# SP's transfers in the order of emission, in a two-layer diffusion transformer on one core

## The chip, the core and the metric

The kernel runs on one core of one Trainium2 chip, in one launch. The metric is the device time of one execution in microseconds; the median of the runs counts. On a core, TensorE (PE, with its weight loads as PEld), VectorE (DVE), ScalarE (ACT) and GpSimd (POOL) compute, each from a queue of its own that it works through in order. SyncE (SP) issues all DMA transfers of this kernel, also in order: an instruction in SP's queue that waits for a semaphore holds up whatever stands behind it.

## The reference

One latent sequence of 1024 tokens and one context of 256 tokens, 1024 features each, pass through two layers; all is float32. In each layer six vectors (shift, scale and gate, twice) are made from the conditioning, `silu(c) @ ada_w + ada_b`, and then:

```
h = h + g1 * mixer(rms_norm(h) * (1 + sc1) + sh1)
h = h + g2 * swiglu_ffn(rms_norm(h) * (1 + sc2) + sh2)
```

Layer 0's mixer is neighbourhood attention with 16 heads of 64: a query on a 16 x 64 grid sees a window of 8 x 16 with a relative-position bias, and all 256 context keys. The context attends to itself and goes through the FFN too. Layer 1's mixer is grouped-query attention with 16 query and 4 key heads, norms and a rotary embedding on q and k, over all 1280 keys; here only the latent tokens go on. The FFN is `(silu(a) * g) @ w_out` with 2816 hidden features. A last norm gives the output.

## The kernel before

Features lie on the partitions, tokens along the free dimension, in three blocks: latent tokens 0 to 511 (block 0), 512 to 1023 (block 1), the context (block 2, 256 wide). Every large product is done in three passes of a rounded high part and a low part (`hi`, `lo`), so each weight tile that arrives (`wr`, 512 KB) is split in two by ACT and by DVE or POOL (lines 632 and 634). The program is written with a scheduler that places instructions by a model of their times, but over most of it the kernel itself fixes the order of the compute engines: inside `manual_schedule` an engine keeps the order in which its instructions are emitted.

There are five stages. `startup` (line 262) makes the first modulation and norm and the projections of the first head pair; its `manual_schedule` has SP in it too. Then comes the attention of layer 0, in two passes over the heads (three pairs of query tiles per head in the first, two in the second). Each pair goes through the stages S, X, m, e, sc, T, c, s, PV, oc, r and z at the times of a table (`ORDERA`, `ORDERB`, with the length of a pair in ns in `PERIODA`, `PERIODB`). In the table's slots between them (names with an F) `Lanes` puts in background work: loading and splitting weights, the Q, K and V projections of the next head pairs, the rest of layer 0's modulation (`ada_chunks`, with the tile `adaw`), and later the output projection. Then the FFN of layer 0 with layer 1's modulation behind it, the attention of layer 1 (`ORDER1`) and the FFN of layer 1 with the last norm.

The background has a clock of its own, `bg.now`, that runs by the table's times. It says when a step may be emitted: a split of a weight 2500 ns after its load was emitted, a use of `adaw` 4000 ns, of `o32` 3000 ns.

Intermediate results go through DRAM, all by `dma` (line 76), which issues on SP, so that nearly every transfer carries line 81. The ones that matter here:

- `stack_out` (line 705) stores a projected block of Q or K, its high parts and its low parts, as two transfers (`Kd<-qh`, `Kd<-ql`, `Qd<-qh`, `Qd<-ql`, in layer 1 `K1d<-`, `Q1d<-`). The destination has the head first: two heads of 64 rows. `qh` and `ql` have two buffers each. In the first attention the background projects, for head pairs 1 to 7, Q of blocks 0 and 2 and K of all three (V after pairs 2, 4 and 6), then Q of block 1 for the second pass.
- `r` (line 834) adds the two halves of a result on POOL (line 838) and, for the second head of two, moves rows between partitions by two transfers `z<-r`. `z` (line 846) adds them on POOL (lines 850, 851) and stores them, `Od<-z` or `O1d<-z`.
- `load_head` (line 1193), called in the first S of a head's second pair (line 1261), loads the next head's queries and keys (`Qs<-Qd` and six `K<-Kd` in the first pass); `load_v0` and `load_bias` load V (`Vt<-Vd`) and the bias (`braw<-Bd`) in that of its first.
- `out_part0` (line 1167) loads the residual `xr` for a product of the output projection, and `out_add0` adds to it (line 1183).
- `weights` (line 610) emits the next weight load as soon as the split that frees its place has been emitted.

SP's queue was not among those with a fixed order after `startup`: the scheduler placed each transfer where its model had it ready, among the transfers that it had placed before.

```
    top.enter_context(tc.manual_schedule(engines={ET.PE, ET.Activation, ET.DVE, ET.Pool}))

    def stack_out(dst, tmp_hi, tmp_lo, c0, n):
        dma(out=dst[:, 0:64, c0:c0 + n], in_=tmp_hi)
        dma(out=dst[:, 64:128, c0:c0 + n], in_=tmp_lo)
```

Of the kernel before, what the change touches and what calls it, by code (L numbers as in the profile page):

```python
# [18 lines left out]
P = 128  # L19
D = 1024  # L20
KC = D // P                      # feature chunks
GRID_H, GRID_W = 16, 64
LAT, CTX = 1024, 256
BLK = [(0, 512), (512, 512), (1024, 256)]   # token blocks (column, width); the last is the context
# [7 lines left out]
# columns of the packed vector array  # L32
# [40 lines left out]
def _build(tc, nc, I, O, top):  # L73
# [28 lines left out]
    silc = const.tile([P, 16], F32, name="silc")        # silu(c) | silu(c_ctx) as columns  # L102
# [3 lines left out]
    # modulation columns: [.., chunk m, lat|ctx]  # L106
    modA = [const.tile([P, 16, 2], F32, name=f"modA{i}") for i in range(2)]   # sh1 sc1
    modB = [const.tile([P, 32, 2], F32, name=f"modB{i}") for i in range(2)]   # g1 sh2 sc2 g2
# [27 lines left out]
    def norm(tag, src, there, n, tmp, bank, done, direct=0, line=0):  # L136
        """the reciprocal root mean square of a block, from its chunks as they come, then the steps done(rs); the squares
        of the last direct ones go to the tensor engine one by one"""
# [52 lines left out]
    def apply_norm(tag, src, rs, G, sh, ah, al, tmp):  # L191
        """the norm's gain and shift, split into hi and lo"""
# [21 lines left out]
    # DRAM scratch  # L214
# [23 lines left out]
    def exp_ln_tables(after):  # L238
        """the one table set that serves both Exp and Ln, once the last Silu is through"""
        with tc.issue_after(after.ins):  # L240
            s.preload_act_table_set("natural_log_exp_and_others")
# [3 lines left out]
    # ================= layer 0: modulation, first norm =================  # L245
    acts = [None] * 3

    # relative-position bias laid out per (head, query, key tile offset, key)
# [13 lines left out]
    def startup():  # L262
        """the norm of every block and the first projections, issued in the order of emission"""
        ET = mybir.EngineType
        with ExitStack() as ph:
# [10 lines left out]
            def start(at, gen):  # L276
                """the steps of a generator, each after the delay that the one before it gave"""
                heapq.heappush(todo, (at, next(count), gen))
# [56 lines left out]
            # silu(c) as rows on every partition  # L335
# [52 lines left out]
            def modulation(m):  # L388
                """shift on the vector engine, scale on the tensor engine"""
# [17 lines left out]
            def apply0(kc):  # L407
                """a chunk of the first block, already scaled by 1/rms"""
# [23 lines left out]
            def first_qk(b):  # L432
                """keys and queries of the first pair, chunk by chunk in turn"""
# [37 lines left out]
    def ada_chunks(pool, layer, ms, nv, crow, raw, clock=None):  # L471
        """modulation chunks (of 128 columns each) on the vector engine, by halves of the sums; the weights come
        transposed. A step before every product"""
# [20 lines left out]
    class Ring:  # L494
        """places used in turn: one is free when what had it before was given back"""
# [18 lines left out]
    class Temps:  # L514
        """fixed tiles by name, each in use until it is given back"""
# [16 lines left out]
    class Job:  # L532
        """weight units and the generator of the products with them, which may start when the first need are there"""
# [5 lines left out]
    class Lanes:  # L539
        """work in the background of an attention, or on its own, for engines that issue in the order of emission: the  # L540
        products advance by cost, what comes before and after a group of them by one instruction per slot of its
        engine, and only when the step before it should be through"""
# [4 lines left out]
        def __init__(self, third):  # L547
            # weights: two places, and a third one as long as its pool is there
            self.third, self.wx = third, None
            self.rings = dict(w=Ring(3), x=Ring(2))  # L550
            self.lo, self.cap = "GD", 6.0       # engines of the weights' low parts, most credit
            self.main, self.credit, self.now = [], 0.0, 0.0
            self.lines = [], [], []             # by urgency
            self.busy = dict(A=0.0, D=0.0, G=0.0)   # until when an engine takes nothing
            self.enter("weights", self.weights(), 0.0, 1)
# [5 lines left out]
        def follow(self, job, gen):  # L561
            """later products with the same weights"""
            job.heir = self.add(job.tag, [], gen)
            return job.heir
# [33 lines left out]
        def place(self, kind):  # L598
            """a weight unit's tiles"""
# [10 lines left out]
        def weights(self):  # L610
            """the units of the next jobs in turn, each loaded and split into hi and lo"""
# [53 lines left out]
        def tick(self, cost=1.0):  # L665
            """a slot of every engine, outside the attention's table"""
# [51 lines left out]
    def proj_v(psm, pool, ws, dst, tiles=range(10)):  # L718
        """token-major values of four heads, hi and lo side by side per head; of a pair of weight units,
        each with four feature chunks of both"""  # L720
# [20 lines left out]
    QCOL = (0, 768, 512)         # columns of the queries of each block: the first pass of the attention takes two  # L741
# [19 lines left out]
    # One attention unit is 128 queries of one head, a pair of them 256. Its stages are issued in the order of a  # L761
    # table that repeats for every pair, with slots between them for the background work.
# [5 lines left out]
    class Pair:  # L768
        """two units; the context's keys (part 0, of both units in one bank) and the other parts"""
# [64 lines left out]
        def r(self):  # L834
            """sum of the hi and lo columns; of the second head of two, the rows 0-63 and 64-127 change places"""
# [10 lines left out]
        def z(self):  # L846
            """both rows summed into the two heads' 128 features"""
# [7 lines left out]
    class Plan:  # L855
        """the stages of all pairs in the order of their tables"""
# [3 lines left out]
        def __init__(self, phases):  # L860
            """of each phase: period, table, pairs, background products per slot, time until the next"""
# [27 lines left out]
    class Halves:  # L889
        """a block's 8 chunks in two tiles"""  # L890
# [7 lines left out]
    class Ffn:  # L898
        """what is left of a layer's output projection, that of block 1, and the FFN. The norms of the other blocks run
        behind the projection, that of block 1 behind the first products of the others"""  # L900
        def __init__(self, layer, blks, last, resid, g1, g2):
# [15 lines left out]
            if layer == 0:  # L917
                bg.add(tag, out(NJ - 4), lambda job: self.mm2(job, NJ - 4, whole), dst="x")
                # the last products of the context first
# [5 lines left out]
            # the last products of block 0 before those of block 1  # L925
# [14 lines left out]
        def start(self, h, tmp, hp, wx, psp, pool, norm):  # L940
            """with what the attention left; norm(b) gives gain and shift"""
# [70 lines left out]
        def silu(self, j, b, ps, k):  # L1012
# [6 lines left out]
            last = s.activation(sa[:, :n], ps[:, :n], AF.Silu)  # L1019
            self.rings["a"].give(k)  # L1020
            self.gates[j, b] = sa, i
            if (j, b) == (NJ - 1, 1):
                exp_ln_tables(last)
# [48 lines left out]
    # ================= layer 0: neighbourhood attention =================  # L1072
    ET = mybir.EngineType
    acts_o = {}
    with ExitStack() as ph:
# [50 lines left out]
        def finish_v0(ps, dst, tb):  # L1126
            """two token tiles"""
# [9 lines left out]
        # the output projection of the blocks that the first pass serves runs behind the second  # L1137
        def out_split0(b):
            """hi and lo of the heads' results, each as soon as it is written"""
# [53 lines left out]
        def load_head(h, ps):  # L1193
            """queries and keys of one head for one pass; the context's keys come last"""
# [126 lines left out]
        # the weights of the first two are there, the third place is free  # L1321
# [548 lines left out]
```

## Time and profile before

| | us |
|---|---|
| median of 3 runs | 3485.12 |
| lowest and highest | 3480.47, 3489.89 |
| span of the profiled execution | 3479.7 |
| PE busy | 3157.8 |
| DVE busy | 1951.5 |
| ACT busy | 1362.9 |
| POOL busy | 1008.5 |

The span is that from the first to the last instruction of one profiled execution; the median of the runs is 5.4 us above it, and no separate time of the profiled execution is given. Matmuls are pipelined, so a busy PE need not be at its peak. The page's digits show the span in 40 slices of 87 us: the busy share of an engine in tenths, where 9 is 90% or more. In a table of stages the stretch (us from the span's start) is followed by its length, by the busy us of PE, PEld, DVE, ACT and POOL with the number of instructions, by the granted clock of TensorE, by the mean busy share of the 16 DMA engines and by what they moved in GB/s. A row of waits has who waited, for whom, and then the us in total, the number of waits and the longest one. A row of a timeline has start, duration, engine, line, operation, output and input, and in brackets how long the engine sat idle before it and for whom. A row of SP's timeline is the issue of a transfer, not the transfer.

### The profile page before, as it was taken

The numbers are of one execution on the slowest core, as the hardware profiler recorded it, in microseconds if no ns is written. First come the engines' busy times: TensorE is split into PE (matmuls) and PEld (weight loads), VectorE is DVE, ScalarE is ACT, GpSimd is POOL, SyncE is SP. The second block draws the span as 40 slices with busy tenths as digits, with TensorE's granted clock in tenths as the row PEclk, the third lists the DMA queues.
The fourth block names the chain that finished last, engine by engine and source line by source line (L and its number), as shares of the span: only waits on it lengthen the run. The fifth ranks groups of instructions, "written<-read, shape, count | busy, mean of one in ns | idle before, by whom it ended". The sixth has DMA issues, their size and how long they took to land.

```text
span 3479.7 us, 48144 instructions
## 1 busy us (share of the span) xinstructions
PE 3157.8 (91%) x17352; PEld 2706.9 (78%) x17352; DVE 1951.5 (56%) x4147; ACT 1362.9 (39%) x3305; POOL 1008.5 (29%) x959
## 2 busy tenths in 40 slices
PE   6767786868999999999999978999999999999998
PEld 4657685757877888888888767888888788888887
DVE  6347454556767655333333747898897534334335
ACT  3224342446753111111111437898887421121123
POOL 3224343445752000000000414666654200000002
PEclk8878898988999999999999989999999999999999
DMA  6546454556853343111111242333332211111111
GB/s 225 133 146 193 147 165 138 161 178 193 249 175 122 115 132 104 37 37 37 37 37 43 104 129 82 100 93 96 100 100 72 88 55 49 43 55 49 43 55 61
DMA packets 194855, 363.41 MB, mean 104 GB/s; under 512 B 30393, under 2 KB 94265, under 8 KB 192569
## 3 DMA queue, kind: packets, MB, share of 16 engines
q1 hardware_dynamic: 194616, 360.33, 32.8%
q8 instruction: 138, 2.26, 0.3%
q14 instruction: 101, 0.82, 0.1%
HBM read 283.71 MB, written 70.64 MB: 102 GB/s over the span
## 4 chain that ended last, share of the span: by engine, by line
PE 60%; DVE 4%; DMA 3%; ACT 1%; POOL 1%; issue 1%; DVEq 0%; ACTq 0%; POOLq 0%; SPq 0%
PE pg L714 5%; PE pa L714 5%; PE pg L713 5%; PE pg L715 5%; PE pa L715 5%; PE pa L713 5%; PE pm L1056 5%; PE pm L1057 5%; PE pm L1055 5%; PE T L810 3%; PE o L492 3%; PE S L1543 1%; PE S L1544 1%; PE ps L713 1%; PE ps L715 1%; PE ps L714 1%
## 5 line engine op out<-in xcount | busy, mean ns | idle before, releaser
L634 POOL TENSOR_TENSOR wl<-wr,wh 128x512 fp32r<-128x512 f32 x119 | 158.6, 1334 | 1443.6 <-ACT wh L632 1436.0
L803 POOL TENSOR_SCALAR Pt<-Pt,rc 128x1280 f32<-128x1280 f32 (+3 forms) x288 | 298.4, 1036 | 495.7 <-DVE rc L798 208.1
L810 PE MATMUL T<-ident,Pt 128*128 128x128 f32 x1952 | 312.9, 281 | 141.2 <-POOL Pt L803 136.5
L818 ACT CAST pT<-T 128x256 fp32r<-128x256 f32 (+2 forms) x672 | 305.1, 477 | 234.9 <-PE T L810 230.7
L810 PEld LDWEIGHTS T<-ident,Pt 128*128 128x128 f32 x1952 | 241.9, 144 | 198.7 <-POOL Pt L803 148.6
L823 DVE TENSOR_TENSOR pT<-T,pT 128x256 fp32r<-128x256 f32 (+2 forms) x672 | 342.2, 535 | 43.1 <-ACT pT L818 42.6
L632 ACT CAST wh<-wr 128x512 fp32r<-128x512 f32 x334 | 207.7, 623 | 343.3 <-PE pg L714 158.6
L714 PE MATMUL pa<-al,wh 128*128 128x512 f32 (+1 forms) x880 | 325.3, 370 | 6.1 <-POOL al L132 4.8
L1055 PE MATMUL pm<-hh,woh 128*128 128x512 f32 (+1 forms) x912 | 330.4, 362 | 0.0
L1056 PE MATMUL pm<-hl,woh 128*128 128x512 f32 (+1 forms) x912 | 329.4, 361 | 0.0
L1057 PE MATMUL pm<-hh,wol 128*128 128x512 f32 (+1 forms) x912 | 329.3, 361 | 0.0
L1067 DVE SCALAR_TENSOR_TENSOR h<-pm,modB,h 128x512 f32<-128x512 f32 (+1 forms) x368 | 242.4, 662 | 150.3 <-PE pm L1057 150.3
L1019 ACT ACTIVATE sa<-pa 128x512 f32<-128x512 f32 (+1 forms) x110 | 60.9, 554 | 676.6 <-PE pa L715 676.5
L713 PE MATMUL ps<-ah,wh 128*128 128x512 f32 (+1 forms) x688 | 273.4, 397 | 57.7 <-DVE ql L757 20.2
L713 PE MATMUL pa<-ah,wh 128*128 128x512 f32 (+1 forms) x880 | 324.2, 368 | 1.2 <-ACT ah L197 1.2
L713 PE MATMUL pg<-ah,wh 128*128 128x512 f32 (+1 forms) x880 | 325.1, 369 | 0.0
L715 PE MATMUL pa<-ah,wl 128*128 128x512 f32 (+1 forms) x880 | 324.5, 369 | 0.1
L714 PE MATMUL pg<-al,wh 128*128 128x512 f32 (+1 forms) x880 | 324.2, 368 | 0.0
L715 PE MATMUL pg<-ah,wl 128*128 128x512 f32 (+1 forms) x880 | 323.7, 368 | 0.0
L492 PE MATMUL o<-pT,Vt 128*128 128x256 f32 x1952 | 298.9, 292 | 9.6 <-DVE rc L797 8.6
L1031 DVE TENSOR_TENSOR sa<-sa,pg 128x512 f32<-128x512 f32 (+1 forms) x110 | 69.8, 634 | 392.1 <-PE pg L715 392.1
L634 DVE TENSOR_TENSOR wl<-wr,wh 128x512 fp32r<-128x512 f32 x215 | 170.2, 792 | 206.0 <-ACT wh L632 205.7
(260 smaller groups left out, 7397.5 us busy)
## 6 DMA issues: line engine op xcount, KB each, us to landing
wr<-in_fin SPq DMA_DIRECT2D x88, 512.0 KB
adaw<-in_adaT SPq DMA_DIRECT2D x160, 256.0 KB
wr<-in_wqkv SPq DMA_DIRECT2D x53, 512.0 KB
wr<-in_fout SPq DMA_DIRECT2D x44, 512.0 KB
wr<-in_wo SPq DMA_DIRECT2D x32, 512.0 KB
z<-r SPq DMA_DIRECT2D x144, 64.0 KB
aw<-in_ada0n SPq DMA_DIRECT2D x8, 1024.0 KB
Qs<-Q1d SPq DMA_DIRECT2D x32, 256.0 KB
```

The source lines that it names most:

```text
L492: t.matmul(o_ap, lhsT=u.V[:, kb, :], rhs=u.pT[:, i, :], start=i == 0, stop=i == len(u.blocks) - 1)
L634: (g if self.engine == "G" else v).tensor_tensor(lo[:, c], raw[:, c], hi[:, c].bitcast(F32), ALU.subtract)
L713: t.matmul(ps, lhsT=hi[:, c], rhs=ah[:, kc, :n], start=kc == 0, stop=False)
L714: t.matmul(ps, lhsT=hi[:, c], rhs=al[:, kc, :n], start=False, stop=False)
L715: t.matmul(ps, lhsT=lo[:, c], rhs=ah[:, kc, :n], start=False, stop=kc == KC - 1)
L803: g.tensor_scalar(Pt, Pt, u.rc[:, 2:3], 1.0, ALU.mult, ALU.mult)
L810: t.transpose(T[:, i * P:(i + 1) * P], u.Pt[:, (i0 + i) * P:(i0 + i + 1) * P], ident[:])
L818: s.copy(u.pT[:, i0:i0 + n, :P], u.T[c])
L823: v.tensor_tensor(u.pT[:, i0:i0 + n, P:], u.T[c], u.pT[:, i0:i0 + n, :P].bitcast(F32), ALU.subtract)
L1055: t.matmul(ps[:, :n], lhsT=hi[:, c], rhs=hh[:, cols], start=i == 0, stop=False)
L1056: t.matmul(ps[:, :n], lhsT=hi[:, c], rhs=hl[:, cols], start=False, stop=False)
L1057: t.matmul(ps[:, :n], lhsT=lo[:, c], rhs=hh[:, cols], start=False, stop=i == 1)
```

## The change

From the start of layer 0's attention to the end of the program, SP is put among the engines that keep the order of emission. With it, the preload of the table set that serves Exp and Ln, behind the last Silu of an FFN, is emitted without the explicit edge to that Silu. The rest of the diff takes out comments and docstrings.

```
     def exp_ln_tables(after):
...
-        with tc.issue_after(after.ins):
+        with tc.issue_after(after.ins) if after else ExitStack():
             s.preload_act_table_set("natural_log_exp_and_others")
...
             sa = self.tmp.tile([P, 512], F32, name="sa", bufs=2)
-            last = s.activation(sa[:, :n], ps[:, :n], AF.Silu)
+            s.activation(sa[:, :n], ps[:, :n], AF.Silu)
...
             if (j, b) == (NJ - 1, 1):
-                exp_ln_tables(last)
+                exp_ln_tables(None)
...
         crow = load_crow(pb)
-        top.enter_context(tc.manual_schedule(engines={ET.PE, ET.Activation, ET.DVE, ET.Pool}))
+        top.enter_context(tc.manual_schedule(engines={ET.PE, ET.Activation, ET.DVE, ET.Pool, ET.SP}))
         bg.enter("bias", bias(0, 0))
```

More of the change, by code (lines that the diff above doesn't have):

```diff
@@ L238, in exp_ln_tables @@
     def exp_ln_tables(after):
-        with tc.issue_after(after.ins):
+        with tc.issue_after(after.ins) if after else ExitStack():
             s.preload_act_table_set("natural_log_exp_and_others")
@@ L1018, in silu @@
             sa = self.tmp.tile([P, 512], F32, name="sa", bufs=2)
-            last = s.activation(sa[:, :n], ps[:, :n], AF.Silu)
+            s.activation(sa[:, :n], ps[:, :n], AF.Silu)
             self.rings["a"].give(k)
@@ L1022, in silu @@
             if (j, b) == (NJ - 1, 1):
-                exp_ln_tables(last)
+                exp_ln_tables(None)
         def gate(self, j, b, ps, k):
@@ L1338, in _build @@
         crow = load_crow(pb)
-        top.enter_context(tc.manual_schedule(engines={ET.PE, ET.Activation, ET.DVE, ET.Pool}))
+        top.enter_context(tc.manual_schedule(engines={ET.PE, ET.Activation, ET.DVE, ET.Pool, ET.SP}))
         bg.enter("bias", bias(0, 0))
```

## The prediction

> **What bounds the kernel now.** I read the page first, then the table of stages (busy time of each engine by stretch of time).
>
> ```profile
> span 3479.7 us, 48144 instructions
> PE 3157.8 (91%) x17352; PEld 2706.9 (78%) x17352; DVE 1951.5 (56%) x4147; ACT 1362.9 (39%) x3305; POOL 1008.5 (29%) x959
> PE   6767786868999999999999978999999999999998
> ...
> 160.00:280.00 120.00, 74.24 (x407) 67.09 (x406) 45.84 (x127) 28.41 (x82) 27.10 (x30) 0.77 0.46 151
> 280.00:320.00 40.00, 38.66 (x305) 37.46 (x304) 34.84 (x93) 18.44 (x56) 17.33 (x20) 1.00 0.68 209
> 320.00:440.00 120.00, 83.73 (x478) 74.04 (x476) 61.31 (x176) 41.46 (x121) 45.96 (x52) 0.86 0.49 153
> 440.00:480.00 40.00, 39.69 (x298) 38.63 (x299) 26.64 (x79) 18.56 (x56) 19.43 (x23) 0.96 0.63 193
> 480.00:600.00 120.00, 81.96 (x485) 72.98 (x484) 53.23 (x156) 40.84 (x120) 43.83 (x49) 0.83 0.42 134
> 600.00:640.00 40.00, 37.98 (x294) 36.58 (x294) 26.68 (x78) 15.72 (x46) 16.76 (x19) 1.00 0.72 232
> 640.00:840.00 200.00, 139.39 (x769) 119.69 (x767) 113.49 (x343) 95.46 (x282) 91.53 (x105) 0.87 0.51 159
> 840.00:960.00 120.00, 114.17 (x788) 104.27 (x789) 91.66 (x323) 90.70 (x278) 87.72 (x103) 0.97 0.86 251
> 1080.00:1920.00 840.00, 840.00 (x4402) 725.13 (x4402) 376.24 (x702) 133.09 (x249) 67.81 (x51) 1.00 0.22 70
> 2160.00:2680.00 520.00, 510.94 (x3433) 448.91 (x3432) 461.71 (x1061) 453.85 (x1196) 317.42 (x284) 1.00 0.32 95
> 2760.00:3440.00 680.00, 680.00 (x2999) 563.25 (x2998) 259.39 (x352) 128.48 (x223) 34.08 (x26) 1.00 0.15 48
> ...
> 960.00:1080.00 120.00, 111.03 (x557) 90.28 (x556) 83.29 (x146) 67.42 (x137) 61.31 (x56) 0.99 0.45 143
> 1920.00:2040.00 120.00, 108.29 (x591) 92.39 (x591) 82.89 (x116) 57.34 (x107) 44.70 (x36) 0.96 0.29 100
> 2040.00:2160.00 120.00, 92.89 (x491) 74.72 (x490) 69.52 (x150) 67.30 (x168) 41.52 (x34) 0.89 0.35 101
> 2680.00:2760.00 80.00, 73.01 (x301) 56.06 (x301) 54.66 (x68) 40.11 (x63) 26.41 (x19) 0.99 0.31 103
> ```
>
> The columns after the stretch are PE, PEld, DVE, ACT and POOL busy, the granted clock, the DMA share and GB/s. Both FFNs (1080 to 1920, 2760 to 3440) keep PE busy for all 840 and 680 us, and the second attention for 510.94 of 520: no order of transfers shortens those. What is left is the first attention, where PE stands idle for over a quarter of 160 to 280, 320 to 440, 480 to 600 and 640 to 840, and no other engine is full either. The three stretches of 40 us between them run PE at 38.66, 39.69 and 37.98. The code tells them apart: in the long stretches the background projects Q and K (two head pairs in each 120 us), in the short ones V. Q and K go out through `stack_out`; here is what its stores do.
>
> ```profile
> Kd<-qh SPq DMA_DIRECT2D x16, 256.0 KB
> ...
> Kd<-qh SPq DMA_DIRECT2D x8, 128.0 KB
> ...
> 516.60 0.55 SPq L81 DMA_DIRECT2D Kd<-qh  x1
> 517.25 4.99 SPq L81 DMA_DIRECT2D Kd<-ql  x1
> ...
> 520.00:522.00 2.00, 1.35 (x6) 0.75 (x4) 0.00 (x0) 0.00 (x0) 0.01 (x1) 1.00 0.13 51
> 522.00:524.00 2.00, 1.04 (x9) 0.92 (x9) 1.52 (x4) 0.00 (x0) 0.00 (x0) 1.00 0.13 52
> 524.00:526.00 2.00, 2.00 (x20) 2.00 (x18) 1.64 (x5) 1.21 (x4) 0.00 (x0) 1.00 0.13 50
> ```
>
> With two stores under way the DMA share is 0.13: two of 16 engines, at 51 GB/s together. A 256 KB store therefore takes 262,144 B / 51 GB/s = 5.1 us and a 128 KB one 2.6 us, one after the other, on two engines that also carry a sixteenth of everything else at 25.5 GB/s. Two head pairs make 6 blocks of 512 and 4 of 256 columns, two stores each: 12 x 5.14 + 8 x 2.57 = 82 us, 4.2 MB. From 160 to 280 the rest is 151 GB/s x 120 us - 4.2 = 13.9 MB, or 34 us on each engine: 116 of 120 us. The same sum gives 117 of 120 (320 to 440), 111 of 120 (480 to 600), and with 20 wide and 4 narrow stores 113 + 64 = 177 of 200 (640 to 840). These stretches are bound by the volume on two DMA engines, and an order does not change a volume.
>
> The Trainium skill ("DMA: Bandwidth & Descriptors", section "Why a DMA increments its semaphore by 16 and not by 1") says that the slowest dimension sets how many engines a DMA gets, always the lowest-numbered. By it all these stores (outermost dimension 2) share one pair, as the sum has it; no row names an engine. Were successive stores on different pairs, the term of 82 us would fall to 41 and the first rival below would lead.
>
> **The change part by part.** The set of engines whose instructions keep the order of emission gets SP, from the first attention to the end. It adds and removes no transfer: the same stores, loads, waits and bytes. `startup` issues SP in order already, so there nothing moves. The loads of the first head, masks, bias and `crow` are emitted ahead of that line and stay with the scheduler. `exp_ln_tables(None)` drops an ordering edge to the last Silu on ACT, which keeps the order of emission anyway: nothing.
>
> What moves lies in SP's queue. A load or store now stands where the code emits it: `z<-r` right behind its add on POOL, the next head's seven loads together, each weight load behind the split that freed its place. What the present order costs shows in the engines' waits from 160 to 840.
>
> ```profile
> POOL z L851 <- DMA z<-r: 122.8, 21, 20.3
> DVE adaj L487 <- DMA adaw<-in_adaT: 75.3, 12, 17.0
> ...
> DVE ql L757 <- DMA Kd<-ql: 25.6, 6, 9.7
> DVE ql L757 <- DMA Qd<-ql: 25.6, 4, 11.0
> ACT qh L755 <- DMA Kd<-qh: 22.1, 4, 8.9
> ACT qh L755 <- DMA Qd<-qh: 10.7, 3, 7.5
> ...
> 531.81 0.72 POOL L838 TENSOR_TENSOR r<-ob 128x256 f32<-128x256 f32 x1 [4.28 <-ACT ob L832]
> 560.76 0.72 POOL L851 TENSOR_TENSOR z<-z,r 64x256 f32<-64x256 f32 x1 [20.29 <-DMA z<-r]
> ...
> 551.46 0.55 SPq L81 DMA_DIRECT2D z<-r  x1
> ```
>
> The longest: r is ready at 532.53, its transfer is issued at 551.46, and POOL sits for 20.29 us. Emission order takes 18.9 us off that delay, and of POOL's 122.8 us I expect well over half to go. But time that the attention wins there it loses at the next two rows' kind: the projections come round sooner and wait for `qh` and `ql` (84 us now), whose two buffers are held by the stores. What is late next is the same pair of DMA engines. The gain is bounded by their gaps: 4 + 3 + 9 + 23 = 38 us; from below it is 0. I take 8, a fifth, because the gaps lie mostly in 640 to 840, where a head of the second pass waits for its own queries. In the V stretches (3.7 us of PE's time missing), the second pass (5.8 of 120) and the second attention (9 of 520) I take 0; what hides the edit there is PE's own work, and without that cover those figures are the most that can move, either way. In the last four rows of the table of stages PE misses 9, 12, 27 and 7 us, at chains of norm, projection, store and load that no queue order shortens: 0, with a quarter of the 27 as bound.
>
> Against it stands one new wait. SP now stops at each `Od<-z` from its place in the code until POOL's z add is through, and every load behind it stops too: K, Q and V of the next head, `adaw`, weights. SP stops there today as well.
>
> ```profile
> SPq L81 <- POOL z L851: 58.7, 18, 8.4
> ...
> 2681.92 2.14 DMA z<-r
> 2684.95 1.86 DMA O1d<-z
> ```
>
> 18 waits of 3.3 us in 160 to 840, and 3.03 us from the issue of one `z<-r` to that of the store behind it on the chain of waits. The table `ORDERA` puts z 3.85 us of its own clock behind r (18183 - 14333 ns), with other transfers emitted between, so most stops should be no longer than now. I take 4 us for all, between 0 and the rival's price below. Sum: span 3479.7 - 8 + 4 = 3475.7. The median of the runs is 5.4 us above the span, so **3481 us**.
>
> **The rivals.** First, the late transfers were the cause. If the two engines were not the limit, 160 to 840 would go at the V stretches' PE share, 116.3 of 120: PE's 495.7 us of work there would take 511 instead of 680. Half of that is 84 us: 3401. For it: the first wait above is the largest of the stage. Against it: the sums of 116, 117 and 111 of 120. Chance 0.11.
>
> Second, the gaps close. Half of the 38 us and a quarter of the 27: 26 us, 3455. For it: nothing waits behind a load that the scheduler put ahead. Chance 0.25.
>
> Third, SP's stops starve the two engines (slower). When the stop at `Od<-z` outlasts what is queued on the two engines (one block's two stores, 10.3 us), they run dry until POOL is through and the next stores are issued. The first pass has 24 such stores; if half run dry for the 3.03 us of that round trip, 36 us: 3517. For it: z has 3.85 us of the table's clock, less than one block's stores. Against it: the same stop exists now. Chance 0.16.
>
> Fourth, loads come too late (slower). The scheduler sends loads as soon as their buffer is free.
>
> ```profile
> 249.63 0.65 SPq L81 DMA_DIRECT2D xr<-in_x  x1
> ...
> L1183 DVE SCALAR_TENSOR_TENSOR xr<-ps,modB,xr x16: 474/612/751, 835.1 to 989.5; 128x512 f32<-128x512 f32 x8, 128x256 f32<-128x256 f32 x8
> ```
>
> The first `xr` is loaded 585 us before its use; in emission order its notice is one product group. The code counts on 4 us for `adaw` and 2.5 for weights, by its own clock. Twelve more waits like those of `adaw` are 75 us, less the 38 of gaps: 37 us, 3518. Chance 0.10. The Trainium skill ("DMA: Bandwidth & Descriptors", section "Rules for kernel authors") says to issue a DMA early and wait late, which speaks against this change; the trace bears it out little, since `adaw` waits 75.3 us under the early order.
>
> Fifth, the order hardly changes, the scheduler having modelled about the order of emission: 3485, chance 0.04; the 18.9 us by which a ready `z<-r` stood back speak against it.
>
> **How the numbers follow.** The forecast of 3481, with its own range of 3471 to 3492, has 0.34. A measurement of this kernel can tell about 0.3%, 10.5 us, from no change. Faster: 0.11 + 0.25 = 0.36. Same: 0.34 + 0.04 = 0.38. Slower: 0.16 + 0.10 = 0.26. The range of 3435 to 3525 takes in the closing gaps and both slower rivals' prices; outside are the first rival and some 0.06 of longer stops.
>
> **What would show it.** In the changed profile SP's timeline has both `z<-r` behind each other and a head's K loads in one row; POOL's wait at L851 falls under 60 us in 160 to 840, and the waits of `ql` and `qh` grow by about as much. A Q and K stretch still takes 113 to 122 us at a DMA share near 0.46. Wrong would be: such a stretch under 105 us (the two engines did not bound it), PE under full in an FFN, or stretches in which the share falls under 0.12 while SP waits for POOL (starved).

## The result, and the profile after

The changed kernel takes 3590.68 us (median of 4 runs, 3587.61 to 3593.12) against 3486.1 us of the kernel before beside it (4 runs): a ratio of 1.0302 with a 95% interval of 1.0286 to 1.0319, 105 us slower. The forecast was 3481 us with a range up to 3525. The profiled execution has a span of 3588.6 us, 108.9 more than before. On its page the busy times of DVE, ACT and POOL hardly differ from those of before. PE's grew by 39.2 us for the same 17352 products, with the mean granted clock at 0.944 instead of 0.957. Its digits have more sixes and sevens ahead of the first FFN.

```profile
span 3588.6 us, 48040 instructions
...
PE 3197.0 (89%) x17352; PEld 2737.8 (76%) x17352; DVE 1944.5 (54%) x4147; ACT 1363.3 (38%) x3305; POOL 999.7 (28%) x959
...
PE   5766686767999999999999977999999899999998
```

The table of stages of the changed kernel, its stretches moved by as much as the stage had moved:

```profile
280.00:360.00 80.00, 58.66 (x391) 55.49 (x392) 42.24 (x127) 28.10 (x83) 29.43 (x37) 0.86 0.50 155
360.00:480.00 120.00, 85.76 (x491) 76.68 (x490) 54.17 (x164) 38.27 (x112) 39.15 (x48) 0.86 0.46 143
520.00:640.00 120.00, 85.45 (x522) 77.13 (x521) 51.95 (x158) 39.49 (x117) 39.76 (x47) 0.84 0.45 145
1140.00:2025.00 885.00, 884.06 (x4617) 761.95 (x4616) 406.85 (x743) 154.98 (x290) 88.04 (x71) 1.00 0.21 69
2240.00:2766.00 526.00, 499.23 (x3271) 438.03 (x3271) 443.84 (x1022) 434.65 (x1145) 301.59 (x269) 0.97 0.31 89
2846.00:3560.00 714.00, 710.86 (x3151) 587.42 (x3150) 280.97 (x385) 148.72 (x253) 45.79 (x35) 1.00 0.15 47
```

The FFNs are as full as before, and the Q and K stretches still take about their 120 us at a DMA share of 0.45. What has changed is the first V stretch, once 40 us at a share of 0.68 and now some 75 at 0.50; the second pass of the first attention; and the second attention. The two rows here are the second pass, first of the kernel before, then of the changed one:

```profile
766.00:972.00 206.00, 181.81 (x1201) 164.79 (x1200) 145.89 (x505) 141.06 (x431) 134.59 (x158) 0.95 0.74 218
```

```profile
798.00:1030.00 232.00, 192.19 (x1199) 172.35 (x1199) 147.53 (x503) 141.46 (x431) 134.06 (x158) 0.91 0.65 197
```

Two marks in the traces show where the time is lost: the first product of each FFN. The first FFN's starts at 1043.6 us before and 1102.3 after, 58.7 later; the second's at 2736.1 and 2845.8, so 51.1 more is lost between the two, and nothing after. Of the 58.7 us, 30 go in the first V stretch and 26 in the second pass (206 us have become 232). The 51.1 are 2 in the first FFN, 8 in the start of the second attention, 34 in its steady part and 7 at its end.

SP's timeline in the first V stretch shows how (start, duration, then output and input; a row with a count takes in the wait between its transfers):

```profile
283.80 9.05 SPq L81 DMA_DIRECT2D adaw<-in_adaT  x2
292.90 1.16 SPq L81 DMA_DIRECT2D z<-r  x2
294.15 1.00 SPq L81 DMA_DIRECT2D Vt<-Vd  x2
...
297.63 10.46 SPq L81 DMA_DIRECT2D adaw<-in_adaT  x2
308.14 1.11 SPq L81 DMA_DIRECT2D z<-r  x2
...
309.93 3.35 SPq L81 DMA_DIRECT2D K<-Kd  x6
```

SP stands for 9 to 10 us between two loads of `adaw`, and `z<-r`, V and K are behind it. The reason is in the code. Two generators, `ada0(16, 24)` and `ada0(24, 48)`, run side by side, each two tiles ahead, and `adaw` has three buffers. The fourth load is emitted before the product that frees its buffer. The scheduler could put it behind other transfers; the order of emission can't. What comes of it can be followed up to PE. In this stretch (278 to 347 us) POOL waits 38.4 us for `z<-r`, and PE waits for `Pt`, which POOL makes; before (270 to 325 us) the two waits were 17.0 and 12.4 us.

```profile
POOL z L850 <- DMA z<-r: 38.4, 3, 20.0
PE T L810 <- POOL Pt L803: 28.4, 3, 17.8
```

SP's waits in the first attention, first before (100 to 960 us), then after (100 to 1030 us; for whom, total, times, longest):

```profile
SPq L81 <- POOL z L851: 69.0, 25, 8.4
...
SPq L81 <- DVE rawB L487: 19.5, 22, 3.2
```

```profile
SPq L81 <- DVE rawB L487: 85.3, 19, 9.3
SPq L81 <- POOL z L851: 62.8, 20, 8.2
SPq L81 <- POOL r L838: 33.9, 22, 3.5
```

### The profile page after: what moved, and what is told of

It reads as the page before. It is cut to its first block, busy times and chain, and to the rows that moved or that the text cites. A ratio compares the mean times of both kernels' runs of the same rounds, so it can differ in the third digit from the quotient of the medians.

```text
span 3588.6 us, 48040 instructions
## 1 busy us (share of the span) xinstructions
PE 3197.0 (89%) x17352; PEld 2737.8 (76%) x17352; DVE 1944.5 (54%) x4147; ACT 1363.3 (38%) x3305; POOL 999.7 (28%) x959
## 3 DMA queue, kind: packets, MB, share of 16 engines
q1 hardware_dynamic: 194616, 360.33, 31.9%
## 4 chain that ended last, share of the span: by engine, by line
PE 57%; DVE 5%; DMA 3%; ACT 1%; issue 1%; POOL 1%; SPq 0%; DVEq 0%; POOLq 0%; ACTq 0%
PE pg L713 5%; PE pg L714 5%; PE pg L715 5%; PE pa L714 5%; PE pa L715 5%; PE pa L713 5%; PE pm L1056 5%; PE pm L1055 5%; PE pm L1057 5%; PE T L810 3%; PE o L492 3%; PE S L1543 1%; PE S L1544 1%; DVE nm L1535 1%; DVE pT L823 1%
## 5 line engine op out<-in xcount | busy, mean ns | idle before, releaser
L810 PE MATMUL T<-ident,Pt 128*128 128x128 f32 x1952 | 323.8, 288 | 154.5 <-POOL Pt L803 138.3
L803 POOL TENSOR_SCALAR Pt<-Pt,rc 128x1280 f32<-128x1280 f32 (+3 forms) x288 | 296.5, 1030 | 535.8 <-DVE rc L798 247.2
L810 PEld LDWEIGHTS T<-ident,Pt 128*128 128x128 f32 x1952 | 250.3, 148 | 214.2 <-POOL Pt L803 150.9
L492 PEld LDWEIGHTS o<-pT,Vt 128*128 128x128 f32 x1952 | 263.7, 196 | 25.4 <-DVE pT L823 12.3
```

Source lines behind the costliest of these rows:

```text
L492: t.matmul(o_ap, lhsT=u.V[:, kb, :], rhs=u.pT[:, i, :], start=i == 0, stop=i == len(u.blocks) - 1)
L803: g.tensor_scalar(Pt, Pt, u.rc[:, 2:3], 1.0, ALU.mult, ALU.mult)
L810: t.transpose(T[:, i * P:(i + 1) * P], u.Pt[:, (i0 + i) * P:(i0 + i + 1) * P], ident[:])
```

## The experiments

Line numbers in rows of experiments are shifted by what was added above them. A row that names only `L81` is SP's `dma`. "After" in a diff is the changed kernel.

### Taking single stops away

The first theory was that transfers are held up behind SP's stops. Rival A was that loads come late for want of early issue, rival B that the stops at the z stores do it. The edit of the first run:

```
         def ada0(lo, hi):
+            while lo == 24 and bg.pending("g1"):
+                yield ""
             yield from ada_chunks(
```

> The modulation's second stream of loads (24 of the 32 chunks) starts only when the first has ended, so that 2 tiles of adaw and not 4 are asked for at once from 3 buffers; everything else as in the changed kernel. Theory (SP stands in its order at an adaw load whose buffer isn't free, and z<-r, K, V and Q loads stand behind it): SP's waits for the adaw products on DVE fall from 76.9 us to under 20, the second pass starts near 775 us instead of 798, time 3561 to 3571. Rival A (loads come late because they are no longer sent ahead): adaw is asked for no earlier and at half the rate, so 3590 or more. Rival B (the stops at Od<-z and O1d<-z): nothing of them changes, 3590.

Measured: 3553.72 us (1.0203, 1.0184 to 1.0223), 37 us less than the changed kernel and somewhat below what was expected. The second pass starts at 759.4 us, 7 before that of the kernel before, and the first FFN's first product 36.8 earlier than in the changed kernel. SP's wait for the products is gone:

```profile
SPq L81 <- DVE rawB L487: 4.3, 5, 1.9
```

Loads that are asked for later made the kernel faster, so rival A isn't what happens in the first pass, and B isn't either. The second pass didn't gain (234.7 us; the single stream now ran on into it).

```
# in weights(), from the start of the second attention: a load is emitted only when
+            self.now >= self.hold        # hold = time of the last split + 6000
```

> From the prologue of the second attention to its end, each weight load is emitted 6 us of the table's clock after the split that frees its buffer, instead of right behind it; a few of the compute instructions around the splits move by a slot. Theory (SP stands at a weight load until DVE has done the split, and the queries' load stands right behind it): SP's waits for wl on DVE in the second attention fall from 120 us to under 40, the second attention gets back 25 to 45 us, time 3545 to 3566. Rival A (loads come late): weights come 6 us later still, so 3590 to 3610. Rival B (stops at the z stores): 3590.

Measured: 3580.93 us (1.0282, 1.0261 to 1.0304), 10 us less. SP's waits for `wl` fell as expected, from 128.0 us (2080 to 2766 us) to 9.0, but those for r rose from 131.9 to 163.5 and those for z from 104.5 to 137.5: SP went on to the next stop. The size of the theory failed here.

```profile
SPq L81 <- POOL r L847: 163.5, 30, 17.8
SPq L81 <- POOL z L860: 137.5, 29, 9.9
```

```
 def z(self): ...
-                dma(out=self.out[...]..., in_=z[:]); self.written.add(...)
+                late_z.append(self)       # stored at the start of the next oc()
```

> Each Od<-z and O1d<-z is emitted with the next oc of the tables, about 3 us of the table's clock behind the add on POOL that it waits for, in both attentions. Theory: SP's waits for z on POOL fall by more than half, but they stood in the kernel before as well, so only the second pass of the first attention gains: 3576 to 3590. Rival B (these stops are the cause, the third rival of the prediction at a larger price): most of the 105 us comes back, 3490 to 3540. Rival A: 3590.

Measured: 3589.4 us (1.0295, 1.0276 to 1.0315): nothing. Again one wait took the other's place (z 104.5 to 33.1 us, r 131.9 to 202.7 in the second attention). So rival B, which was the prediction's slower rival, is out for the stops at the stores of z by themselves. What all of SP's stops cost together this run doesn't show, since they only changed places.

```
# SP in manual_schedule only until layer 0's FFN has ended:
+    order.close()
+    top.enter_context(tc.manual_schedule(engines={PE, Activation, DVE, Pool}))
```

> SP keeps the order of emission only until layer 0's FFN has ended; from the prologue of the second attention on the scheduler places the transfers again. Theory and all rivals that act where they stand: the first attention's loss of 59 us stays, with the FFN's 2, and what came after it (47 us) goes: 3545 to 3552. If the later loss were passed on from the first attention (another phase of weights or banks), 3575 to 3590; if the first attention's loss were the scheduler's doing because it can't move transfers from the later stages ahead, under 3530.

Measured: 3542.64 us (1.0169, 1.0151 to 1.0186). The first FFN's first product comes 57.4 us late and the second's 58.5: each part loses its own time, about half and half.

### The second pass, and POOL's queue

```
                     if self.i == 0: load_v0(h, ps); load_bias(nxt[0])
-                    elif self.i == 1 and nxt[1] < 2: load_head(*nxt); ...
+                    if self.i == 1 - ps and nxt[1] < 2: load_head(*nxt)
```

> In the second pass of the first attention the next head's Qs and K loads are emitted in the first S of the head before instead of its second, one pair (5.56 us of the table) earlier; the compute engines' orders stay as they are. Theory, as it stands after the first four runs (what hurts is a load with little notice behind a stop of SP): PE's waits for K in the second pass (21.0 us at the first product, 12.6 at the second) fall under 10, and the second pass, which lost 26 us, gets 12 to 26 back: 3565 to 3579. Rival C (the second pass lost at the output projection's own chain, Od<-z, o<-Od, xr): 3585 to 3592.

Measured: 3577.43 us (1.0273, 1.0255 to 1.0291), 13 us less, and the second pass takes 217.2 us where the changed kernel's takes 231.6 and the kernel before's 205.5. PE's waits for K in the second pass, after and in this run:

```profile
PE S L1269 <- DMA K<-Kd: 21.0, 8, 8.6
PE S L1270 <- DMA K<-Kd: 12.6, 11, 2.3
```

```profile
PE S L1271 <- DMA K<-Kd: 8.2, 10, 1.6
...
PE S L1270 <- DMA K<-Kd: 7.1, 4, 3.4
```

One pair more of notice brings back over half of the 26 us. The loads also stand elsewhere among SP's stops now, and the run doesn't tell the two apart.

```
-                dma(out=self.z_[0:64, :], in_=...)       # and the other z<-r, and the z store
+                dma(out=self.z_[0:64, :], in_=..., queue=nc.gpsimd)
```

> z<-r, Od<-z and O1d<-z are issued from POOL's own queue, right behind the adds that they wait for, so that SP has none of them; SP keeps the order of emission for the rest. Theory (a transfer held up by SP's stops is what makes the queries and keys late): the second attention's loss of 34 us goes almost whole, and part of the second pass's 26: 3535 to 3560, if issuing costs POOL no more than the 0.5 us that it costs SP. Rival D (only the stops at adaw and wl matter, those at r and z cost nothing because SP came to them early): 3585 to 3592. Above 3595 POOL's own time for the issue would be the bound.

Measured: 3565.79 us (1.0239, 1.0217 to 1.0261), 25 us less, all of it in the first attention: the first FFN starts 30 us earlier than in the changed kernel, and from there to the second FFN it takes 1750.0 us instead of 1743.5. In the first pass `z<-r` no longer stood behind `adaw`, and that won most of what e1 had won by taking the stop away. The first V stretch shows it, here in this run (270 to 336 us): SP still stands at `adaw`, but POOL hardly waits for `z<-r`.

```profile
SPq L81 <- DVE rawB L487: 31.2, 6, 8.3
POOL z L850 <- DMA z<-r: 3.6, 1, 3.6
```

In e1 POOL's wait there is 3.2 us, in the changed kernel 38.4. So what the first V stretch lost is `z<-r` queued behind `adaw`. The sum over the whole first pass would not show that: 119.3 us in the changed kernel, 95.3 in e1 and 31.9 here, but 109.9 before, with no such loss. In the second attention the theory failed again, SP standing at `wl` instead:

```profile
SPq L81 <- DVE wl L634: 284.9, 20, 22.0
SPq L81 <- DMA O1d<-z: 102.8, 10, 17.6
```

### The two engines of the stores

```
-        dma(out=dst[:, 0:64, c0:c0 + n], in_=tmp_hi)        # the same for tmp_lo
+        for a in range(2): dma(out=dst[a, 0:64, c0:c0 + n], in_=tmp_hi[64 * a:64 * a + 64])
```

> The kernel before, with each store of stack_out sent as two transfers of 64 rows, one for each head, instead of one whose outermost dimension is 2. The prediction's reading (the two engines that these stores get bound the Q and K stretches of the first attention): the DMA share in those stretches is no longer held by two engines, 160 to 840 gives back 40 to 84 us: 3400 to 3445. Rival E (those stretches wait for chains of latency, not for the two engines): 3470 to 3490.

Measured: 3227.4 us (0.9267, 0.9251 to 0.9283), 254 us less than the kernel before and three times the most that was expected. No other edit here comes near it, and it is the version to keep. Its Q and K stretches:

```profile
140.00:260.00 120.00, 109.44 (x766) 101.07 (x765) 96.64 (x268) 57.40 (x172) 58.98 (x66) 1.00 0.78 240
160.00:400.00 240.00, 229.53 (x1596) 212.48 (x1597) 190.31 (x532) 123.29 (x366) 131.54 (x147) 1.00 0.76 229
```

PE is busy for 229.53 of 240 us with the share at 0.76 and no stretches of two kinds any more. The prediction's reading of the bound was right, and its price for lifting it (84 us) too small by far. The kernel before says the same of the bound when it is read microsecond by microsecond: in 359 of the 360 us of its three Q and K stretches ahead of 600 us the DMA share is at least 0.12, that of two engines, and in 129 of them no more than 0.15.

> The same stores in the changed kernel. By the prediction's reading the first attention gives back the same 40 to 84 us here, and in the second attention the low part's store no longer stands 5.1 us behind the high part's when SP held the high part's back: some 10 to 30 us of its 34: 3480 to 3540. If the loss were all in SP's stops and the two engines bound nothing: 3580 to 3592.

Measured: 3320.31 us (0.9534, 0.9515 to 0.9552), 270 less than the changed kernel and far below what was expected. But e8 stands 93 us behind e7: the order's loss hardly shrinks with the bound lifted, 60.3 of it ahead of the first FFN and 34.9 between the FFNs (51.1 with the slow stores). So a part of the second attention's loss went with its slow stores; most did not.

### Four edits together, and their control

> The changed kernel with four edits to what stands in SP's order: adaw is asked for only when one of its 3 buffers is free by the order of emission (both streams stay), weight loads of the second attention 6 us later (as in e2), heads of the second pass a pair earlier (as in e5), z<-r and the z stores on POOL's queue (as in e6). Theory (the whole loss is transfers held up behind stops of SP, in three places): under 15 us of the first attention's 59 are left and under 8 of the second's 34: 3485 to 3515. If a cause that isn't named yet holds a good part: over 3535.

> The changed kernel with two of the four: weight loads of the second attention later, and z<-r and the z stores on POOL's queue. Theory (in e6 SP only went from one stop to the next and stood at wl for 285 us with the queries behind it; in e2 at r for 163 us): with both away the second attention's 34 us shrink under 10, and the time is that of e6 less 20 to 30: 3535 to 3548. Rival F (the queries are late because the low part's store of Q1d lands late, on its two engines, whatever SP does): 3555 to 3568.

> e9 with the stores of stack_out on all engines as in e8. Theory (e8 stood 93 us behind e7 for the same stops): the stops gone, the order of emission is as good as the scheduler's, 3220 to 3250. If the scheduler's order has a merit of its own beside avoiding stops: over 3265.

> The four edits of e9 in the kernel before, where the scheduler places the transfers (the table preload without its edge, as in the changed kernel). It had these transfers out of the way already: 3470 to 3495. Well under that, the edits would be gains of their own, and what e9 gains would not all be the order's loss.

The edits of e2, e5 and e6, and for `adaw` one ring of three places for both streams (e12 has all of it without `ET.SP`):

```
-            while todo and len(tiles) < 2:
+            while todo and len(tiles) < 2 and ring.free():     # ring = Ring(3), given back
                                                                # behind the products
```

The two last columns are from the traces: the start of the first FFN's first product, and the time from there to the second's.

| run | us | ratio, 95% interval | first FFN starts | first FFN to second |
|---|---|---|---|---|
| before | | | 1043.6 | 1692.5 |
| after | 3590.68 | 1.0302, 1.0286 to 1.0319 | 1102.3 | 1743.5 |
| e9 | 3524.22 | 1.0118, 1.0101 to 1.0135 | 1033.5 | 1748.6 |
| e10 | 3565.6 | 1.0234, 1.0214 to 1.0254 | 1076.8 | 1742.4 |
| e12 | 3489.85 | 1.0014, 1.0005 to 1.0024 | 1041.8 | 1706.4 |
| e11 | 3320.3 | 0.9536, 0.9517 to 0.9555 | 865.4 | 1707.8 |
| e7 | 3227.4 | 0.9267, 0.9251 to 0.9283 | 815.8 | 1663.6 |

Only e12 came out as expected; e9 missed its theory's range by 9 us, e10 fell into rival F's, and e11 stands far above its theory's. The first attention's loss is gone in e9, and the second's untouched, in e9 as in e10. SP had no stop at r or z there any more, but it was not free either: in e9's second attention it stood at `wl`, whose loads had been moved, and for POOL's stores of z to land (`O1d<-z`).

```profile
SPq L81 <- DVE wl L648: 170.5, 13, 20.7
SPq L81 <- DMA O1d<-z: 113.9, 10, 17.6
```

So these runs did not take SP's stops out of the second attention, and what a queue without stops would win there stays open. The edits have a price of their own too: the control e12 is as fast as the kernel before as a whole, but from FFN to FFN it takes 14 us more. POOL is busy for 1122.0 us there instead of 1008.5. With the fast stores POOL's queue costs time in the first attention. e11 and e15 (below) have the same edits there, but for POOL's queue; the first FFN starts at 865.4 us in e11 and at 836.1 in e15 (with the slow stores POOL's queue won time: 1033.5 in e9, 1049.7 in e14). PE waits for POOL's `Pt` (140 to 600 us), e11 and e15:

```profile
PE T L825 <- POOL Pt L818: 48.6, 27, 5.1
```

```profile
PE T L816 <- POOL Pt L809: 23.3, 22, 3.7
```

In e8, with the stops at `adaw`, this wait is 44.3 us. So e11 took the stops away, paid for POOL's issues instead, and is no faster than e8.

### Notice in the second attention

SP's stops alone tell little here. In the second attention, before (2067 to 2680 us) and after (2137 to 2783 us), those at r (152.3 and 131.9 us) and z (112.8 and 109.2 us) have not grown; only those at `wl` have:

```profile
SPq L81 <- DVE wl L634: 46.5, 17, 9.2
```

```profile
SPq L81 <- DVE wl L634: 131.9, 21, 15.6
```

Both traces show the loads of K for head 8 and the product that needs them first, before (issued at 2167.82 to 2169.89 for 2240.00) and after (at 2305.38 for 2317.05):

```profile
2167.82 0.45 SPq L81 DMA_DIRECT2D K<-K1d  x1
...
2168.78 1.11 SPq L81 DMA_DIRECT2D K<-K1d  x2
...
2240.00 0.39 PE L1527 MATMUL X<-K,Qs 128*128 128x256 f32 x1
```

```profile
2305.38 1.58 SPq L81 DMA_DIRECT2D K<-K1d  x3
2307.01 0.60 SPq L81 DMA_DIRECT2D Vt<-V1d  x1
2307.71 0.38 SPq L81 DMA_DIRECT2D Qs<-Q1d  x1
...
2317.05 0.55 PE L1527 MATMUL X<-K,Qs 128*128 128x256 f32 x1 [4.57 <-issue]
```

The scheduler sends them as soon as the other of the two buffers is free, 72 us ahead; in the order of emission it is 12, and PE stands 4.57 us. The row names no load as what ended this wait; that it is these loads, the next run shows. PE stands where other groups of four heads begin too (10.7 us at head 4, where the row names `Qs<-Q1d`, the queries' load), and at two places ACT waits for `o<-O1d` and PE behind it (4.8 and 5.1 us).

```
+            if self.b % 4 == 2 and self.h % 4 == 1 and key != (13, 1):
+                heads1["next"] = load_kv((self.h + 3) % HEADS)     # K, V of the next group
# e13_kv_q_o_notice also: head_setup1 from the head's first pair; in out_split
-            ready = bg.now + 3000
+            ready = bg.now + 8000
```

> The changed kernel with the K and V loads of each new group of four heads in the second attention emitted two heads earlier (about 33 us); all compute orders as they are. Theory, restated after the runs so far (in the second attention it isn't SP's stops but the notice: at every fourth head K, V and Q, some 2.2 MB, are asked for one pair of 8.2 us ahead): the stalls at the first X of those heads (10.7, 4.6 and 3.6 us) go or shrink: 3569 to 3581. Rival H (stops of SP ahead of the queries, whatever their notice): 3587 to 3593.

Measured: 3582.3 us (1.0278, 1.0251 to 1.0305), 8 us less, between the theory's range and rival H's; from FFN to FFN 1732.5 us. The stall at head 8 is gone, that at head 4 is still 7.1 us.

> As the one before, and the queries' loads a pair earlier where their projection is through, and the results read back (o<-O1d) given 8 us of the table's clock before ACT splits them, instead of 3 (the output projection moves by a few slots). Theory of notice: ACT's waits for o<-O1d (13.5 us, and two stalls of 4.8 and 5.1 us of PE behind them) go too: 3553 to 3571, with under 14 of the second attention's 34 us left. Rival H: 3585 to 3593.

Measured: 3573.31 us (1.0265, 1.0246 to 1.0284), 17 us less; 1726.9 from FFN to FFN. Rival H is out as the whole cause, but the theory is short by a few us: ACT's waits for `o<-O1d` stayed (13.6 us). The next theory was that SP comes to these loads late because it stands at `wl`, for 138.2 us from 2060 to 2800.

```profile
ACT wh L632 <- DMA wr<-in_wqkv: 17.9, 1, 17.9
ACT ah L1575 <- DMA o<-O1d: 13.6, 4, 7.6
```

> The changed kernel with adaw asked for only when a buffer is free by the order of emission, heads of the second pass a pair earlier, and the three of the run before; POOL's queue and the weight loads are left as they are. Theory (two causes: a load asked for without a free buffer stops SP in the first pass; everywhere else the order of emission gives loads too little notice): 3490 to 3530. If stops at r, z and wl do hold a part: 3535 to 3560.

Measured: 3521.14 us (1.0116, 1.0098 to 1.0134), 70 us less, as expected: the first FFN starts 6.0 us later than before, and from there to the second it takes 1726.6 us. The control for the two edits in the first attention is e12. Those of e13 were not run in the kernel before, so that they are no gains of their own there is not shown.

> The run before with stack_out's stores on all engines. The changed kernel with that edit alone stood 93 us behind the kernel before with it, and the four edits with POOL's queue moved nothing there, because POOL's issues cost PE 40 us of waits for Pt in the first attention. Theory: without POOL's queue 55 to 75 of the 93 us come back: 3245 to 3268. If the scheduler has a merit beside free buffers and notice: over 3290.

Measured: 3255.54 us (0.9349, 0.9334 to 0.9365), as expected: 65 of the 93 us between e8 and e7.

```
     live["att"] = True
+    bg.defer = 6000.0        # the hold of e2, from here to the attention's end
```

> e14 with the weight loads of the second attention (not of its prologue) 6 us of the table's clock later. Theory (with the notice mended, what is left between the first FFN's start and the second's, 34 us, is o<-O1d and queries held behind SP's stop at wl): SP's waits for wl in the second attention fall from 102 us to under 40 and 8 to 18 us come back: 3503 to 3514. If stops at wl cost nothing once there is notice: 3518 to 3526.

Measured: 3507.13 us (1.0068, 1.0047 to 1.0088), 14 us less than e14 and as expected; 1718.2 us from FFN to FFN. The waits for `o<-O1d` stayed even so (14.1 us in e14, 13.4 here), so that part of the theory failed. SP's waits for `wl` in the second attention, e14 and e16:

```profile
SPq L81 <- DVE wl L640: 102.1, 19, 13.1
```

```profile
SPq L81 <- DVE wl L648: 16.3, 3, 8.7
```

> The same edit in e15, with the stores on all engines. Theory: of the 28 us to the kernel before with such stores 5 to 10 come back: 3245 to 3251. If the rest is in the second pass and the start of the second attention, where this edit does nothing: 3253 to 3258.

Measured: 3247.22 us (0.932, 0.9302 to 0.9338), 8 us less than e15, as expected. Of the 105 us, edits to what stands where in SP's order bring back 84; 22 are left in e16, and 20 in e17 against e7. From FFN to FFN e16 is 25.7 us behind the kernel before, but e17 (1671.2 us) only 7.6 behind e7: most of what is left there goes with the slow stores, as rival F has it. One stall of the rest is known: a weight load that lands late in the start of the second attention holds ACT and then PE, in the changed kernel for 15.9 us (5.2 before) and in e16 still:

```profile
PE T L1477 <- ACT sq L1473: 15.2, 1, 15.2
```

Why these stores cost more in the order of emission wasn't tried, and so it is open whether the rest is stops or notice.

## Why the prediction was wrong, step by step

- **What bounds the kernel.** Right, and shown by e7: the stores on two engines bound the Q and K stretches. They still take about 120 us with the order changed, none fell under 105, and the first rival (late transfers were the cause) didn't come. The price was mis-sized: 84 us for half of the way to the V stretches' pace, where e7 won 254. Of these some 34 were won ahead of the first attention's first product and 29 between the FFNs; the rest, over 190, fell in the first attention, where the whole way that the sum had, from 680 to 511 us, is 169.
- **The gain at `z<-r`, 8 us.** It failed. POOL's wait did not fall from 122.8 under 60 us. It moved to line 850, since both `z<-r` are now emitted together, and is 119.3 us in the first pass, 109.9 before: emitted right behind its add, the transfer still stood behind SP's stops, at `adaw` in the first V stretch and at others elsewhere (95.3 us are left in e1, without those at `adaw`). So the price set against it, longer waits for `qh` and `ql`, did not come either (84 us from 160 to 840 before, 81 from 160 to 872 after).
- **"The new wait", 4 us.** This is the step that failed most. I named what SP stops at as `Od<-z` and priced only that; e3 shows that to move those stops is worth nothing. The stop that came was at `adaw`, 85.3 us instead of 19.5, and it cost some 30 us. The row for it was there before, and the code has four tiles asked for in three buffers; I read `adaw` as a matter of notice (4 us of the clock), not of a buffer that is not free. e1 and e6 both remove its price, each from another end.
- **"In the V stretches, the second pass and the second attention I take 0."** It failed: 30, 26 and 34 us, and 17 more around the FFNs. I said that the few us in which PE was idle "are the most that can move, either way". PE's idle time bounds a gain, as long as its own work takes the same time. It doesn't bound a loss: the cover that I named, PE's own work, depends on queries and keys being there, and the early issue was part of what put them there (72 us of notice for K at head 8, then 12). In the same sentence I left out that PE's own work takes longer at a lower clock: its busy time grew by 39.2 us.
- **The rivals.** The mechanism of the third (stops starve the two engines) is not what happened: with the stores taken off the two engines the order still costs 93 us (e8 against e7). That of the fourth (loads come too late, chance 0.10) is a part of it: loads emitted earlier win 13 us in e5 and 17 in e13. Its price, 37 us, took notice only at `adaw`, where the cause was another, and took off 38 us of gaps that didn't close. The Trainium skill ("DMA: Bandwidth & Descriptors", "Rules for kernel authors") says to issue early and wait late, and the runs agree where I had weighed the rule low: 72 us of notice became 12, and a longer notice again took the 4.57 us at head 8 away.
- **The range.** It ended at 3525 because the slower rivals were priced one by one. The outcome was two causes at once, each larger than priced: a stop at a buffer that isn't free in the first pass, short notice for a part of the rest. Of the 51.1 us between the FFNs, notice brings back 17 and the moved weight loads 8 more; 26 stay without a shown cause.

## What to carry to other kernels

Before a queue is put into the order of emission, go through its transfers one by one: is the buffer free, by the same order, when the load is emitted, and how much earlier than its use does the old schedule issue it? A transfer that has to wait takes everything behind it along. Removing one such stop can merely move the queue to the next, as in e2, e3 and the second attention of e6, so notice and free buffers are best mended together. And idle time of the busiest engine bounds what can be won as long as its own work takes the same time, never what can be lost.

## What the runs showed of the hardware

A store with two heads outermost runs on two DMA engines, at 51 GB/s. Sent as two of 64 rows, the same bytes let the stage move 229 GB/s, and the kernel went from 3482 to 3227 us: three times what I had made of the volume on those engines. The granted clock of TensorE goes with it. This is the changed kernel:

```profile
160.00:280.00 120.00, 72.14 (x384) 63.20 (x382) 43.02 (x120) 26.20 (x75) 20.25 (x24) 0.78 0.40 129
```

Against the row 140 to 260 of e7 above: with PE busy 72.14 of 120 us the granted clock is 0.78, with 109.44 it is 1.00. In these rows the stage that leaves PE idle also runs its products at a lower clock. How much of the 254 us that is wasn't measured by itself; PE's busy time for the same 17352 products is 3100.9 us in e7 instead of 3157.8, at a mean clock of 0.992 instead of 0.957. The Trainium skill ("TensorE: Matmul & The Clock Gate", "Part 1: The HAM clock gate") says that the clock is held back by default and that activity releases it; the rows agree.

POOL can issue transfers, but not for nothing: in e12 it has 215 more instructions and 113.5 us more busy time (1122.0 - 1008.5), about half a microsecond each.
